# Fixed slots and an urgent first gather for the sample's index tiles, a third key/value buffer, counts by immediates, and a norm step with scalars

## The chip, the cores and the metric

The kernel runs on one core of one Trainium2 chip. The core has a matrix engine (TensorE, "PE" in the profile; "PEld" is its loading of stationary tiles), a vector engine (VectorE, "DVE"), a scalar engine (ScalarE, "ACT"), a general engine (GpSimd, "POOL") and a queue that issues most transfers (SyncE, "SP"). Each engine works through its own list of instructions in order and waits on semaphores for the others. The metric is the device time of one execution in microseconds, lower is better. Times of a kernel are medians over several executions; the profile shows one further execution.

## What is computed

One decoder layer for 1024 prompt tokens and for 8 sequences of 4 sample tokens that have 8192 cached tokens each. The inputs are normalised and projected once for two parallel groups of heads. Group A attends to the 256 best keys that a small "indexer" picks, group B is a retention with a running state. Both are gated, joined, projected, normalised, added to the input, and a gated embedding is added.

```python
def _rmsnorm(x, g):
    xf = x.astype(jnp.float32)
    y = xf * lax.rsqrt(jnp.mean(xf * xf, axis=-1, keepdims=True) + EPS) * g.astype(jnp.float32)
    return y.astype(x.dtype)

def _index_select(qi, wi, ki, qpos, kpos, topk):
    s = jnp.einsum('bqhd,bsd->bqhs', qi.astype(jnp.float32), ki.astype(jnp.float32)) * (D_IDX ** -0.5)
    score = jnp.einsum('bqh,bqhs->bqs', wi.astype(jnp.float32), jax.nn.relu(s))
    valid = kpos[None, None, :] <= qpos[None, :, None]
    score = jnp.where(valid, score, -jnp.inf)
    top_val, top_idx = lax.top_k(score, topk)
    return top_idx, jnp.isfinite(top_val)

def _dsa_sample(qa, ka, va, qi, ki, wi, cache_k, cache_v, cache_kidx, page_table, rel_bias):
    ...
    ki_past = cache_kidx[page_table].reshape(B, past, D_IDX).astype(ki.dtype)
    ki_all = jnp.concatenate([ki_past, ki], axis=1)
    ...
    idx, ok = _index_select(qi, wi, ki_all, qpos, kpos, topk)
    ...
```

## The kernel before

Matrix products are done in float32 by three products of split operands (`xh`, `xl` and `whi`, `wlo`): a weight block is loaded as `wraw`, cast by ACT to `whi` (L179), and POOL subtracts to get `wlo` (L181, four instructions for each half of a block). The program lists what is to be done; a scheduler that knows the dependences and the buffers sets the order on each engine, mostly by the order of the code. A tile belongs to a pool and a tag; a tag has a number of buffers, and an instruction that writes a reused buffer waits for the buffer's last readers, a store among them.

The stages that matter here, in order of time:

- *Start.* Nine blocks of tokens are loaded and normalised. `rstd_of` (L233) computes the inverse root of the mean square: ACT's `Sqrt`, a reciprocal, and one Newton step on DVE (L241 to L244, tiles of 128x1). The row is scaled (L532), transposed by PE into `pt` (L223) and split into `xh` (ACT, L228) and `xl` (DVE, L229). The same helper serves the output norm in `finish_y` (L1691).
- *Projections.* `proj_b` (L248) runs three matmuls per 128 rows of weights over three groups of tokens (`GRP`: 384, 384 and 288). Its results `pb` are consumed by `use_qa`, `use_ka`, `use_va`, `use_ga`. `use_kv` (L402) copies the keys or values of a group to `kvs` (ACT, L406), transposes them on PE (`kvt`, L410), copies them back (DVE, L412) and stores them. `kvs`, `kst`, `qst` and `sga` share the tag `qst` with two buffers.
- *Prompt selection.* Scores of the prompt's blocks are summed on DVE (L502) and masked by POOL (`score`, L504). `bisect_prompt` (L631) finds the 256th largest score of each row bit by bit. It copies the upper halves of the scores to 16 bits (`mask`, L668, one copy a block), counts once against zero, and then makes 15 rounds. A round counts six blocks: the two longest on ACT (`js`, L657), the others on DVE (`jk`, L661). ACT's sums of signs become counts by one step on the two columns (L665, with a constant table `cst`). Then `gb` (L680) and the next candidate `cand` (L682) follow. Every count of the next round waits for `cand`.
- *Sample index.* 16 gathers (L799, one per half of a sequence) bring cached index keys to `kx`, two buffers. PE transposes each in two halves (`ptx`, L809), ACT copies a half to `kT` (L810), PE multiplies it by the index queries (`pox`, L813), ACT applies the ReLU to `rl` (L816), and four `rl` are summed over heads with the weights `wst` on PE (`py`, L772 and L775), copied to `ys` (L777), stored, and transposed to `xe` (L784, L788). All these tiles come from the pool `sx` with rotating tags. The loop also advances the bisection and the rest of the projections (`unit`). Ahead of the loop stand `wst` (L756, from `wcol`) and the newest keys' scores: `pn`, `rn` (L762), `newsc` (L763 to L766).

Of the kernel before, what the change touches and what calls it, by code (L numbers as in the profile page):

```python
# [10 lines left out]
F32 = mybir.dt.float32  # L11
F32R = mybir.dt.float32r
# [108 lines left out]
def tile_step(ctx: ExitStack, tc: tile.TileContext, I, O):  # L121
# [32 lines left out]
    def C(name, rows=128):  # L154
        o, w = _CW[name]
        return cst[:rows, o:o + w]
# [76 lines left out]
    def rstd_of(ss, rows, scale, name, sp):  # L233

        v = sp.tile(list(ss.shape), F32, tag="rs_v", bufs=2, name=f"rv_{name}")
        nc.vector.tensor_scalar(v[:rows], ss[:rows], scale, EPS, op0=ALU.mult, op1=ALU.add)
        y = sp.tile(list(ss.shape), F32, tag="rs_y", bufs=2, name=f"ry_{name}")
        z = sp.tile(list(ss.shape), F32, tag="rs_z", bufs=2, name=f"rz_{name}")
        nc.scalar.activation(y[:rows], v[:rows], AF.Sqrt)
        nc.vector.reciprocal(y[:rows], y[:rows])  # L240
        nc.vector.tensor_tensor(z[:rows], y[:rows], y[:rows], op=ALU.mult)  # L241
        nc.vector.tensor_tensor(z[:rows], z[:rows], v[:rows], op=ALU.mult)
        nc.vector.tensor_scalar(z[:rows], z[:rows], -0.5, 1.5, op0=ALU.mult, op1=ALU.add)
        nc.vector.tensor_tensor(y[:rows], y[:rows], z[:rows], op=ALU.mult)  # L244
        return y
# [155 lines left out]

    def use_kv(g, pt, outs, outp, new):  # L402

        t0, n = GRP[g]
        st = qsp.tile([128, 2, 384], F32, tag="qst", bufs=2, name="kvs")
        nc.scalar.copy(st[:, 0, :n], pt[:, :n])  # L406
        tp = bank("kvt", "t")
        for i in range(0, n, 128):
            rows = min(128, n - i)
            nc.tensor.transpose(tp[:rows, i:i + 128], st[:, 0, i:i + rows], ident)  # L410
        nb = min(n, T - t0)
        nc.vector.tensor_copy(st[:, 1, :nb], tp[:, :nb])  # L412
        tk = st[:, 1, :nb].rearrange("p (b c) -> p b c", c=128)
        nc.sync.dma_start(outp[0, 0, t0:t0 + nb].rearrange("(b p) n d -> p b (n d)", p=128), tk)
        if g == 2:
            nc.vector.tensor_copy(new, tp[:NS, 256:384])
            nc.sync.dma_start(outs.rearrange("o b t n d -> (o b t) (n d)"), new)
        return tk
# [49 lines left out]
    with pool("ix", side="right") as ix:  # L468
# [69 lines left out]

        warm = ix.tile([128, 1], F32, name="warm")
# [15 lines left out]
        def project(g):  # L555

            proj_b(wki, 0, 72, use_ki, (g,))
            qis = ix.tile([128, 8, 384], F32R, tag="qis", bufs=2, name=f"qis{g}")
# [72 lines left out]
    def bisect_prompt():  # L631
# [18 lines left out]
        def count(src, thr, op, scale=None):  # L650
# [12 lines left out]
            if scale:  # L663
                a = slice(NB - NA, NB)
                V.scalar_tensor_tensor(cnt[:, a], cnt[:, a], -0.5, C("halfn")[:, a], op0=ALU.mult, op1=ALU.add)  # L665
# [82 lines left out]
    sx = sxs.enter_context(pool("sx", side="right"))  # L748

    wcol = sx.tile([128, 8], F32, name="wcol")  # L750
    wst = sx.tile([128, 8, 32], F32, name="wst")
    nc.sync.dma_start(wi_d, wi[:NS, 8, :])
# [8 lines left out]
    rn = sx.tile([NS, 8, NS], F32, name="rn")  # L761
# [7 lines left out]
    def head_sum(b, rls):  # L769
# [6 lines left out]
        ys = sx.tile([128, 512], F32, tag="ys", bufs=2, name="ys")  # L776
# [4 lines left out]
    def by_key(b, ys):  # L781
# [3 lines left out]
        xe = sx.tile([128, 4, 4, 4, 4], F32, tag="xe", bufs=1, name="xe")  # L785
# [9 lines left out]
    for b in range(8):  # L795
        rls = []
        for a in range(2):
            kx = sx.tile([128, 2048], F32, tag="kx", bufs=2, name="kx")
            nc.gpsimd.indirect_dma_start(  # L799
                out=kx, out_offset=None, in_=pages,  # L800
                in_offset=bass.IndirectOffsetOnAxis(ap=kidx[:, a * 8 + b:a * 8 + b + 1], axis=0))
            for up in range(2):
                pt = pair("ptx")
                kT = sx.tile([128, 1024], F32, tag="kT", bufs=2, name="kT")
# [10 lines left out]
                rl = sx.tile([128, 512], F32, tag="rl", bufs=6, name="rl")  # L815
# [1012 lines left out]
```

## Time and profile before

| | us |
|---|---|
| median of 3 runs | 1053.49 |
| lowest and highest | 1051.36, 1053.96 |
| the profiled execution's own time | 1057.99 |
| its span, first to last instruction | 1056.2 |
| granted PE clock, mean over the span | 0.977 |

The profiled execution lies 4.5 us above the median, and 1.8 us of its time lie outside the span. A group of the profile is written as line, engine, operation, the tile written and the tiles read (buffer numbers left out). In a timeline a row has the start, the duration, what ran, how often, and in brackets how long the engine had idled and what ended that. In a table of stretches PEclk is the clock that PE was granted, 1.00 being full.

### The profile page before, as it was taken

Reading aid. Unit: us, or ns where it says so; the run is one execution under the profiler, and the core shown is the slowest. Engines: PE = TensorE matmul, PEld = TensorE weight load, DVE = VectorE, ACT = ScalarE, POOL = GpSimd, SP = SyncE. Lnnn points to the kernel's source line nnn. Section 1 sums busy time; section 2 is a strip of 40 time slices with the busy share of each in tenths; the row PEclk is TensorE's granted clock in tenths of the full one; section 3 lists DMA queues with packets and bytes.
Section 4 is the critical chain, followed back from the end, with each engine's and each line's share of the span. In section 5 each row is a group of like instructions: output and inputs, shape, how many; then the busy total and the mean of one; then the engine's idle time right before and its main releaser. Section 6 shows DMA issues by size and latency. Waiting matters only on the chain.

```text
span 1056.2 us, 19867 instructions
## 1 busy us (share of the span) xinstructions
PE 994.1 (94%) x7375; PEld 836.9 (79%) x7375; DVE 678.7 (64%) x2022; ACT 504.2 (48%) x1092; POOL 322.6 (31%) x425
## 2 busy tenths in 40 slices
PE   4999998998999799998999996899999999999998
PEld 3999997766776798887888883566665899999998
DVE  6847678888492466977959937687754423773332
ACT  6546455876434377632252435556644523442211
POOL 4204123120301433525644512544330432232200
PEclk9999998998999899999999996999999999999999
DMA  8211236545353311202201724523211312432211
GB/s 294 66 60 51 95 96 208 185 130 173 123 165 108 74 42 41 61 23 87 65 22 52 180 75 136 151 76 107 79 56 42 117 41 81 136 126 87 82 38 40
DMA packets 98309, 102.24 MB, mean 97 GB/s; under 512 B 21346, under 2 KB 88386, under 8 KB 95906
## 3 DMA queue, kind: packets, MB, share of 16 engines
q1 hardware_dynamic: 92450, 74.74, 23.6%
q0 software_dynamic: 5760, 26.22, 7.9%
q8 instruction: 58, 0.95, 0.4%
q14 instruction: 41, 0.34, 0.1%
HBM read 79.25 MB, written 21.68 MB: 96 GB/s over the span
## 4 chain that ended last, share of the span: by engine, by line
PE 44%; DVE 5%; DMA 2%; POOL 2%; issue 2%; ACT 1%; SPq 0%; ACTq 0%; POOLq 0%; DVEq 0%
PE ptp L1596 4%; PE ob L1604 4%; PE pg L267 3%; PE pg L269 3%; PE pg L268 3%; PE po L267 3%; PE po L268 3%; PE po L269 3%; PE sa L1580 2%; PE sa L1581 2%; PE pvg L268 1%; PE pvg L269 1%; PE pvg L267 1%; PE pty L1651 1%; POOL wlo_vgb L181 1%
## 5 line engine op out<-in xcount | busy, mean ns | idle before, releaser
L1159 POOL DMA_INDIRECT kvs<-in_cache_kv,idx x64 | 66.7, 1042 | 78.8 <-ACT pT L1601 31.7
L267 PE MATMUL pqk<-whi_qkb,xh 128*128 128x256 f32 x256 | 75.1, 293 | 4.4 <-DVE rp L1038 4.3
L267 PE MATMUL pvg<-whi_vgb,xh 128*128 128x256 f32 x256 | 75.5, 295 | 0.5 <-ACT whi_qkb L179 0.4
L268 PE MATMUL pqk<-wlo_qkb,xh 128*128 128x256 f32 x256 | 74.3, 290 | 0.0
L268 PE MATMUL pvg<-wlo_vgb,xh 128*128 128x256 f32 x256 | 74.2, 290 | 0.0
L269 PE MATMUL pqk<-whi_qkb,xl 128*128 128x256 f32 x256 | 73.9, 289 | 0.0
L267 PE MATMUL po<-whi_o,yTh 128*128 128x256 f32 x256 | 73.2, 286 | 0.4 <-ACT yTh L1646 0.4
L269 PE MATMUL pvg<-whi_vgb,xl 128*128 128x256 f32 x256 | 73.5, 287 | 0.0
L267 PE MATMUL pg<-whi_g,yTh 128*128 128x256 f32 x256 | 72.7, 284 | 0.0
L269 PE MATMUL po<-whi_o,yTl 128*128 128x256 f32 x256 | 72.7, 285 | 0.0
L268 PE MATMUL po<-wlo_o,yTh 128*128 128x256 f32 x256 | 72.7, 284 | 0.0
L269 PE MATMUL pg<-whi_g,yTl 128*128 128x256 f32 x256 | 72.3, 283 | 0.0
L268 PE MATMUL pg<-wlo_g,yTh 128*128 128x256 f32 x256 | 72.2, 282 | 0.0
L1589 ACT ACTIVATE L<-L,mn 128x128 f32<-128x128 f32 (+7 forms) x64 | 49.6, 778 | 17.6 <-DVE mn L1586 17.0
L267 PEld LDWEIGHTS pqk<-whi_qkb,xh 128*128 128x128 f32 x256 | 49.4, 193 | 8.2 <-issue 3.5
L502 DVE SCALAR_TENSOR_TENSOR score<-r,wi,score 128x384 f32<-128x384 f32 (+5 forms) x42 | 41.0, 976 | 23.0 <-ACT r L498 21.7
L1785 DVE TENSOR_TENSOR sgm<-pu,sgm 128x256 f32<-128x256 f32 x32 | 13.6, 424 | 64.3 <-PE pu L269 60.6
L181 POOL TENSOR_TENSOR wlo_g<-wraw_g,whi_g 128x256 fp32r<-128x256 f32 x32 | 27.2, 881 | 87.4 <-ACT whi_g L179 87.3
L799 POOL DMA_INDIRECT kx<-in_cache_kidx,kidx x16 | 15.9, 995 | 116.7 <-PE ptx L809 115.8
L269 PEld LDWEIGHTS pqk<-whi_qkb,xl 128*128 128x128 f32 x256 | 49.5, 193 | 2.6 <-issue 2.4
L498 ACT ACTIVATE r<-si 128x384 f32<-128x384 f32 (+5 forms) x48 | 36.3, 758 | 32.0 <-PE si L356 30.6
L267 PEld LDWEIGHTS pvg<-whi_vgb,xh 128*128 128x128 f32 x256 | 48.5, 189 | 3.5 <-issue 0.8
(545 smaller groups left out, 3332.6 us busy)
## 6 DMA issues: line engine op xcount, KB each, us to landing
wraw_qkb<-in_w_in SPq DMA_DIRECT2D x16, 256.0 KB
wraw_vgb<-in_w_in SPq DMA_DIRECT2D x16, 256.0 KB
wraw_o<-in_w_out SPq DMA_DIRECT2D x8, 512.0 KB
qas<-qas_d SPq DMA_DIRECT2D x8, 512.0 KB
xr<-in_x_prompt SPq DMA_DIRECT2D x8, 512.0 KB
wraw_g<-in_w_ple_gate SPq DMA_DIRECT2D x8, 512.0 KB
out_y_prompt<-sgm SPq DMA_DIRECT2D x32, 128.0 KB
qas_d<-qst SPq DMA_DIRECT2D x8, 384.0 KB
```

What stands on the lines that cost most here:

```text
L181: nc.gpsimd.tensor_tensor(lo[:, a * 4 + k, :n], raw[:, k, :n], hi[:, a * 4 + k, :n].bitcast(F32), op=ALU.subtract)
L267: nc.tensor.matmul(pt[:, :n], ah, hi[:, k, :n], start=(k == 0), stop=False)
L268: nc.tensor.matmul(pt[:, :n], ah, lo[:, k, :n], start=False, stop=False)
L269: nc.tensor.matmul(pt[:, :n], al, hi[:, k, :n], start=False, stop=(k == kc - 1))
L498: nc.scalar.activation(r[:, :n], s[:, :n], AF.Relu)
L502: nc.vector.scalar_tensor_tensor(sc, r[:, :n], wi[:, qb, h:h + 1], sc, op0=ALU.mult, op1=ALU.add)
L1159: return nc.gpsimd.indirect_dma_start(out=dst, out_offset=None, in_=kvflat, in_offset=bass.IndirectOffsetOnAxis(ap=idx, axis=0))
L1580: nc.tensor.matmul(s[:, :wc], qas[:, h, :], kah[kv][:, c:c + wc], start=True, stop=False)
L1581: nc.tensor.matmul(s[:, :wc], qas[:, h, :], kal[kv][:, c:c + wc], start=False, stop=True)
L1589: behind[0] = nc.scalar.activation(L[:, :n], L[:, :n], AF.Exp, bias=least, scale=-1.0, accum_out=sm[:, i4:i4 + 1])
L1596: nc.tensor.transpose(tp[:, i4 * 128:i4 * 128 + 128], P[i4][:, kb * 128:kb * 128 + 128], ident)
L1604: nc.tensor.matmul(ob[64 * o:64 * o + 64, :256], vtok[:, kb, kv * 64:kv * 64 + 64], pT[:, o * 256:o * 256 + 256], start=(kb == 0), stop=(k ...
```

## The change

Four edits:

- *Norm step.* Of the three steps with two operands two are fused into one with two scalar operands read per partition, and the third takes its second factor as such a scalar.
- *Third key/value buffer.* For the middle group of tokens `kvs` gets a tag of its own, `kvx`, in the pool `sx`.
- *Counts by immediates.* The step that turns ACT's two sums into counts becomes two steps of one column, each with its constants in the instruction.
- *Sample's index tiles.* `rn`, `xe` and every rotating tile get a fixed slot, all made at the head of the stage in a set order (the first use of a tag takes the tile made then). The order in which they are made sets where they lie. The first two gathers have no wait of their own left, where before they waited for the last readers of the memory under them. The first gather is issued under high priority.

Beside these, the buffer `qis0` is made some lines earlier.

```diff
-        nc.vector.tensor_tensor(z[:rows], y[:rows], y[:rows], op=ALU.mult)
-        nc.vector.tensor_tensor(z[:rows], z[:rows], v[:rows], op=ALU.mult)
+        nc.vector.tensor_scalar(z[:rows], y[:rows], y[:rows], v[:rows], op0=ALU.mult, op1=ALU.mult)
         nc.vector.tensor_scalar(z[:rows], z[:rows], -0.5, 1.5, op0=ALU.mult, op1=ALU.add)
-        nc.vector.tensor_tensor(y[:rows], y[:rows], z[:rows], op=ALU.mult)
+        nc.vector.tensor_scalar(y[:rows], y[:rows], z[:rows], None, op0=ALU.mult)
...
+    sxp = []
+
     def use_kv(g, pt, outs, outp, new):
 
         t0, n = GRP[g]
-        st = qsp.tile([128, 2, 384], F32, tag="qst", bufs=2, name="kvs")
+        st = (sxp[0].tile([128, 2, 384], F32, tag="kvx", bufs=1, name="kvs") if g == 1 else
+              qsp.tile([128, 2, 384], F32, tag="qst", bufs=2, name="kvs"))
...
+        qfirst = ix.tile([128, 8, 384], F32R, tag="qis", bufs=2, name="qis0")
...
             if scale:
-                a = slice(NB - NA, NB)
-                V.scalar_tensor_tensor(cnt[:, a], cnt[:, a], -0.5, C("halfn")[:, a], op0=ALU.mult, op1=ALU.add)
+                for j in range(NB - NA, NB):
+                    V.tensor_scalar(cnt[:, j:j + 1], cnt[:, j:j + 1], -0.5, (j + 3) * 64.0, op0=ALU.mult, op1=ALU.add)
...
     sx = sxs.enter_context(pool("sx", side="right"))
+    sxp.append(sx)
+
+    made = {}
+
+    def slot(tag, shape, name):
+        if tag in made:
+            return made.pop(tag)
+        return sx.tile(shape, F32, tag=tag, bufs=1, name=name)
 
     wcol = sx.tile([128, 8], F32, name="wcol")
     wst = sx.tile([128, 8, 32], F32, name="wst")
+    rn = sx.tile([NS, 8, NS], F32, name="rn")
+    made["xe"] = sx.tile([128, 4, 4, 4, 4], F32, tag="xe", bufs=1, name="xe")
+    for tag, w in (("ys0", 512), ("ys1", 512), *((f"rl{i}", 512) for i in range(1, 6)), ("kT1", 1024),
+                   ("kx1", 2048), ("rl0", 512), ("kT0", 1024), ("kx0", 2048)):
+        made[tag] = sx.tile([128, w], F32, tag=tag, bufs=1, name=tag)
+    turn = {"rl": 0, "kT": 0, "kx": 0, "ys": 0}
+
+    def ring(tag, w, n):
+        i = turn[tag] % n
+        turn[tag] += 1
+        return slot(f"{tag}{i}", [128, w], tag)
+
...
-            kx = sx.tile([128, 2048], F32, tag="kx", bufs=2, name="kx")
-            nc.gpsimd.indirect_dma_start(
-                out=kx, out_offset=None, in_=pages,
-                in_offset=bass.IndirectOffsetOnAxis(ap=kidx[:, a * 8 + b:a * 8 + b + 1], axis=0))
+            kx = ring("kx", 2048, 2)
+            with (tc.high_priority() if b + a == 0 else nullcontext()):
+                nc.gpsimd.indirect_dma_start(
+                    out=kx, out_offset=None, in_=pages,
+                    in_offset=bass.IndirectOffsetOnAxis(ap=kidx[:, a * 8 + b:a * 8 + b + 1], axis=0))
             for up in range(2):
                 pt = pair("ptx")
-                kT = sx.tile([128, 1024], F32, tag="kT", bufs=2, name="kT")
+                kT = ring("kT", 1024, 2)
...
-                rl = sx.tile([128, 512], F32, tag="rl", bufs=6, name="rl")
+                rl = ring("rl", 512, 6)
```

`ys` and `xe` are taken in the same way. The edits also move instructions. On POOL, at the entry of the sample's index, the order before was this (`score` is the select of a prompt block, `kx` a gather, `wlo_ga` one half of the split of the first gate weights):

```order
L504 AFFINE_SELECT score<-score 128x128 x2
L799 DMA kx<-in_cache_kidx,kidx 128x2048 x2
L181 TENSOR_TENSOR wlo_ga_1923<-wraw_ga_1924,whi_ga_1922 128x256 x4
L181 TENSOR_TENSOR wlo_ga_1923<-wraw_ga_1931,whi_ga_1922 128x256 x4
L799 DMA kx<-in_cache_kidx,kidx 128x2048 x6
```

The same place on POOL in the changed kernel:

```order
L506 AFFINE_SELECT score<-score 128x128
L181 TENSOR_TENSOR wlo_ga_1922<-wraw_ga_1923,whi_ga_1921 128x256 x4
L822 DMA kx_1725<-in_cache_kidx,kidx 128x2048
L506 AFFINE_SELECT score<-score 128x128
L822 DMA kx_1722<-in_cache_kidx,kidx 128x2048
L181 TENSOR_TENSOR wlo_ga_1922<-wraw_ga_1930,whi_ga_1921 128x256 x4
L822 DMA kx<-in_cache_kidx,kidx 128x2048 x6
```

The first half of the split moved ahead of the first gather, and the last block's select moved between the two gathers. On DVE, at the same place, before (`mask` is the copy of the last block's scores, `jk` the passes of the first count):

```order
L668 COPY mask<-score 128x1024
L763 TENSOR_TENSOR rn<-rn,wi 32x256
L337 SCALAR_TENSOR_TENSOR qst<-pb,qst 64x384
L661 TENSOR_SCALAR jk,cnt<-mask 128x1024
L764 TENSOR_REDUCE newsc<-rn 32x32
L661 TENSOR_SCALAR jk,cnt<-mask 128x896
L765 TENSOR_TENSOR newsc<-newsc,cst 32x32
L661 TENSOR_SCALAR jk,cnt<-mask 128x768
L766 TENSOR_TENSOR newsc<-newsc,cst 32x32
L661 TENSOR_SCALAR jk,cnt<-mask 128x640
L337 SCALAR_TENSOR_TENSOR qst<-pb,qst 64x256
```

And on DVE in the changed kernel:

```order
L785 TENSOR_TENSOR rn<-rn,wi 32x256
L786 TENSOR_REDUCE newsc<-rn 32x32
L336 SCALAR_TENSOR_TENSOR qst<-pb,qst 64x256
L392 TENSOR_SCALAR qs<-pb 64x32 x2
L787 TENSOR_TENSOR newsc<-newsc,cst 32x32
L788 TENSOR_TENSOR newsc<-newsc,cst 32x32
L427 TENSOR_TENSOR kst<-pb,kst 128x384
L779 TENSOR_TENSOR wst<-wcol,cst 128x256
L671 COPY mask<-score 128x1024
L664 TENSOR_SCALAR jk,cnt<-mask 128x1024
L664 TENSOR_SCALAR jk,cnt<-mask 128x896
```

The last block's copy and the whole first count moved behind the newest keys' scores, `kst` and `wst`. On ACT, from the two casts of the gate weights on, before:

```order
L179 CAST whi_ga_1922<-wraw_ga_1924 128x1024
L179 CAST whi_ga_1922<-wraw_ga_1931 128x1024
L336 ACTIVATE qst<-pb 64x256 x2
L657 ACTIVATE js,cnt<-mask,cand 128x1024
L810 COPY kT<-ptx 128x1024
L657 ACTIVATE js,cnt<-mask,cand 128x896
L810 COPY kT<-ptx 128x1024
L424 CAST kst<-pb 128x384
L816 ACTIVATE rl<-pox 128x512
```

And on ACT in the changed kernel:

```order
L179 CAST whi_ga_1921<-wraw_ga_1923 128x1024
L179 CAST whi_ga_1921<-wraw_ga_1930 128x1024
L335 ACTIVATE qst<-pb 64x256
L784 ACTIVATE rn<-pn 32x256
L335 ACTIVATE qst<-pb 64x256
L426 CAST kst<-pb 128x384
L408 COPY kvs<-pb 128x384
L660 ACTIVATE js,cnt<-mask,cand 128x1024
L660 ACTIVATE js,cnt<-mask,cand 128x896
L833 COPY kT_1724<-ptx 128x1024
```

`rn`, `kst` and `kvs` moved ahead of the first `js`, and both `js` of the first round stand ahead of the first `kT`.

More of the change, by code (lines that the diff above doesn't have):

```diff
@@ L1 @@
 import math
-from contextlib import ExitStack
+from contextlib import ExitStack, nullcontext
 import numpy as np
@@ L557, in project @@
             proj_b(wki, 0, 72, use_ki, (g,))
-            qis = ix.tile([128, 8, 384], F32R, tag="qis", bufs=2, name=f"qis{g}")
+            qis = qfirst if g == 0 else ix.tile([128, 8, 384], F32R, tag="qis", bufs=2, name=f"qis{g}")
             qiss.append(qis)
@@ L760, in tile_step @@
         nc.tensor.matmul(pn[:NS, h * 32:h * 32 + 32], qsn[:, h, :], kis, start=True, stop=True)
-    rn = sx.tile([NS, 8, NS], F32, name="rn")
     nc.scalar.activation(rn, pn[:NS, :256].rearrange("p (h k) -> p h k", h=8), AF.Relu)
@@ L775, in head_sum @@
                 nc.tensor.matmul(py[32 * i:32 * i + 32, :], wst[:, b, :], rls[i], start=True, stop=True)
-        ys = sx.tile([128, 512], F32, tag="ys", bufs=2, name="ys")
+        ys = ring("ys", 512, 2)
         nc.scalar.copy(ys, py)
@@ L784, in by_key @@
             nc.tensor.transpose(pt[:, i * 128:(i + 1) * 128], ys[:, i * 128:(i + 1) * 128], ident)
-        xe = sx.tile([128, 4, 4, 4, 4], F32, tag="xe", bufs=1, name="xe")
+        xe = slot("xe", [128, 4, 4, 4, 4], "xe")
         pv = pt.rearrange("p (r i e) -> p r i e", r=4, i=4)
```

## The prediction

> **What bounds the kernel now.** I read the page's busy shares first, then a table of stretches, then the timeline of each engine inside the stretches in which TensorE (PE) has gaps.
>
> ```profile
> span 1056.2 us, 19867 instructions
> PE 994.1 (94%) x7375; PEld 836.9 (79%) x7375; DVE 678.7 (64%) x2022; ACT 504.2 (48%) x1092; POOL 322.6 (31%) x425
> ```
>
> PE works for 994.1 of 1056.2 us. The change adds and removes no matmul, so it can only act on the 62 us in which PE idles and on the clock that PE is granted after idling. Next, a table of stretches that the edited code touches (from and to; length; busy time and instructions of PE, its weight loads, DVE, ACT and POOL; PE's clock; DMA share; GB/s).
>
> ```profile
> 0.00:22.00 22.00, 7.78 (x29) 5.91 (x30) 13.88 (x35) 13.84 (x27) 10.37 (x18) 1.00 0.89 286
> 178.00:186.00 8.00, 6.04 (x18) 2.49 (x19) 7.71 (x22) 7.43 (x13) 0.28 (x1) 0.57 0.89 320
> 238.00:243.00 5.00, 2.50 (x9) 0.62 (x7) 4.76 (x16) 4.54 (x8) 0.96 (x1) 0.75 0.82 242
> 243.00:248.00 5.00, 4.84 (x20) 2.73 (x24) 3.70 (x15) 4.81 (x9) 0.00 (x0) 0.57 0.90 263
> 902.00:924.00 22.00, 21.09 (x181) 20.70 (x180) 18.40 (x58) 10.60 (x31) 7.89 (x9) 1.00 0.45 142
> ```
>
> Read PE's busy time against the length, then the clock. The start leaves PE empty for 14 us. Around 180 and 240 PE waits, and its clock falls to 0.57 to 0.75 for some microseconds. Around 910 there is under 1 us to win. The three waits in the middle, as PE's timeline has them:
>
> ```profile
> 175.11 1.94 PE L809 MATMUL ptx<-cst,kx 128*128 128x128 f32 x16 [1.09 <-DMA kx<-in_cache_kidx,kidx]
> 179.96 1.97 PE L813 MATMUL pox<-kT,qbd 128*64 128x512 f32 x4 [2.91 <-ACT kT L810]
> 213.06 0.81 PE L410 MATMUL kvt<-cst,kvs 128*128 128x128 f32 x3 [2.76 <-ACT kvs L406]
> 240.96 1.98 PE L813 MATMUL pox<-kT,qbd 128*64 128x512 f32 x4 [2.43 <-DVE vnew L416]
> ```
>
> The first index tile comes late and its copy `kT` later; at 213.06 a key/value copy is late; at 240.96 a VectorE (DVE) copy. Each part of the change aims at one of these or at the start.
>
> **The urgent gather and the late count.** Before, GpSimd (POOL) and the cast on ScalarE (ACT) that it waits for do this:
>
> ```profile
> 167.27 0.29 POOL L504 TENSOR_SCALAR_AFFINE_SELECT score<-score 128x128 f32<-128x128 f32 x1 [20.94 <-DVE score L502]
> 168.14 1.38 POOL L799 DMA_INDIRECT kx<-in_cache_kidx,kidx  x1 [0.57 <-issue]
> 169.67 2.00 ACT L179 CAST whi_ga<-wraw_ga 128x1024 fp32r<-128x1024 f32 x2 [1.36 <-PE pb L258]
> 170.80 5.58 POOL L181 TENSOR_TENSOR wlo_ga<-wraw_ga,whi_ga 128x256 fp32r<-128x256 f32 x8
> ```
>
> The changed order puts half of that weight split, four of the eight, **ahead** of the first gather, and the last score block's select behind the gather. The split waits for the cast, which waits for PE, so it cannot start before 170.80 whatever its place. Its half takes 5.58 / 2 = 2.79, so the first gather is issued at about 173.6 instead of 168.14, 5.5 us later, in spite of its urgency. From issue to PE's use it took 175.11 - 168.14 = 6.97, so `ptx` starts near 180.6. The select follows gather (1.38) and gaps near 175.5.
>
> On DVE the mask copy of that block and the whole first count now stand behind nine other steps, from `rn` (the newest keys' score) to `wst`.
>
> ```profile
> 167.82 0.69 DVE L668 COPY mask<-score 128x1024 bf16<-128x1024 bf16 x1
> 168.43 0.40 DVE L763 TENSOR_TENSOR rn<-rn,wi 32x256 f32<-32x256 f32 x1
> 177.44 0.16 DVE L676 TENSOR_SCALAR cand<-tbits 128x6 int32<-128x6 int32 x1
> 181.21 0.42 DVE L756 TENSOR_TENSOR wst<-wcol,cst 128x256 f32<-128x256 f32 x1
> 169.00:177.00 8.00, 5.32 (x12) 1.00 0.85 290
> ```
>
> The nine (first and last are the second and fourth row) sum to about 3.6 us; in the new order `rn` can begin near 172.5, when ACT has passed the two casts and two short copies, so the mask copy starts near 176.1. Mask 0.69, the count 5.32 (the last row: the count's line alone, six passes and six readouts), 0.5 of small steps: first `cand` at 182.6 against 177.44, **5.2 us later**. ACT's order then has two `js` passes, not one, ahead of the first `kT`:
>
> ```profile
> 177.63 1.15 ACT L657 ACTIVATE js<-mask,cand 128x1024 bf16<-128x1024 bf16 x1 [2.36 <-DVE cand L676]
> 178.90 1.01 ACT L810 COPY kT<-ptx 128x1024 f32<-128x1024 f32 x1
> 179.80 1.04 ACT L657 ACTIVATE js<-mask,cand 128x896 bf16<-128x896 bf16 x1
> ```
>
> 178.90 - 177.63 = 1.27 and then 1.04 put `kT` at 184.9; `pox` follows 1.06 behind it as before, at 186.0 against 179.96: PE loses **6.0 us** here, and the landing at 180.6 is not what decides. What hid the gather before is gone; `kT` is late because of the count.
>
> **The third key/value buffer.** Only the middle token group of the key and value projections gets it.
>
> ```profile
> 212.61 0.40 ACT L406 COPY kvs<-pb 128x288 f32<-128x288 f32 x1 [1.59 <-DMA out_k_prompt<-kvs]
> 201.39 0.53 SPq L426 DMA_DIRECT2D ka_d<-kst  x1
> 205.44 0.39 SPq L414 DMA_DIRECT2D out_k_prompt<-kvs  x1
> 190.76 0.49 PE L410 MATMUL kvt<-cst,kvs 128*128 128x128 f32 x3
> 213.80 3.31 PE L813 MATMUL pox<-kT,qbd 128*64 128x512 f32 x8
> 186.78 1.08 PE L813 MATMUL pox<-kT,qbd 128*64 128x512 f32 x4
> ```
>
> The copy at 212.61 waited for the store issued at 205.44, which took 7.17. Now that copy waits for the `ka_d` store of 201.39, four microseconds older. If it too took 7.17 it is done at 208.6, and PE reaches the transpose at 213.06 - 2.76 = 210.3. So the 2.76 goes, and with it the slow stretch behind it: 0.81 - 0.49 on the transposes and 3.31 - 2 x 1.08 on `pox`, some 1.5. Together 4.3 on PE's own path.
>
> **The count by immediates.** Fifteen two-operand steps become thirty one-operand ones.
>
> ```profile
> 232.32 5.56 POOL L181 TENSOR_TENSOR wlo_ga<-wraw_ga,whi_ga 128x256 fp32r<-128x256 f32 x8
> 234.16 3.75 DVE L665 SCALAR_TENSOR_TENSOR cnt<-cnt,cst 128x2 f32<-128x2 f32 x1 [0.82 <-ACT js L657]
> 240.54 0.27 DVE L416 COPY vnew<-kvt 32x128 f32<-32x128 f32 x1
> L665 DVE SCALAR_TENSOR_TENSOR cnt<-cnt,cst x15: 153/160/3745, 181.5 to 252.1; 128x2 f32<-128x2 f32 x15
> ```
>
> One of fifteen lasted 3745 ns instead of 160, to the end of POOL's run of eight subtractions (232.32 + 5.56 = 237.88), and `vnew`, which PE waits for at 240.96, is queued behind it. The new step has one input from memory. But `cand` two steps on still has two, and falls into the same POOL run. Bounds for what it will wait: 0, or all that is left of the run, about 3.2. The norm's rows below show two-input steps beside POOL at 0.65 and 0.73; they are the many, 3745 the one, so I take 0.6: **3.0 saved** on DVE. Against it 12 rounds up to `vnew` with a second small step, 0.1 each: +1.2. The Trainium skill (SBUF — State Buffer, "Who interferes with whom") says that a DVE instruction with two SBUF inputs contends with a GpSimd instruction that reads SBUF and that the loser waits for the whole instruction. By that rule a wait is at most one subtraction, 5.56 / 8 = 0.70, the 3745 ns are not explained, and the sum would be the one taken here.
>
> **DVE's loop sets the exit.** DVE, ACT and PE are tied round by round here, so the later of two paths counts. DVE's own waits between 178 and 244 (total, times, longest):
>
> ```profile
> DVE cnt L665 <- ACT js L657: 3.5, 5, 1.4
> DVE kvs L412 <- PE kvt L410: 0.8, 1, 0.8
> ```
>
> DVE up to `vnew`: +5.2 entry; -0.8, since `wst` (0.42) and `kst`, put at the same, now lie ahead of the count; -3.0 +1.2 from above; and of the 4.3 us in these two rows I take 2.6 as gone, the 0.8 with PE's gap and half of the 3.5, since the second `js` no longer stands behind `kT` in the first round: **0.0**. Bounds: none of them gone (+2.6), all gone (-1.7). PE's own path: +6.0 -4.3 -2.43 = -0.7, so DVE decides and the stage ends where it did.
>
> **The norm step.** Three two-operand steps become two with a scalar operand.
>
> ```profile
> 12.55 0.73 DVE L241 TENSOR_TENSOR rz_x<-ry_x 128x1 f32<-128x1 f32 x1
> 13.31 0.65 DVE L242 TENSOR_TENSOR rz_x<-rz_x,rv_x 128x1 f32<-128x1 f32 x1
> 13.99 0.15 DVE L243 TENSOR_SCALAR rz_x<-rz_x 128x1 f32<-128x1 f32 x1
> 14.18 0.46 DVE L244 TENSOR_TENSOR ry_x<-ry_x,rz_x 128x1 f32<-128x1 f32 x1
> 17.15 1.94 PE L223 MATMUL pt<-cst,score 128*128 128x128 f32 x8 [3.89 <-DVE xl L229]
> ```
>
> The stretched rows stand beside POOL's work; the 0.15 row, with one memory input, does not stretch. The new third chain is three steps at some 0.19 pitch, 0.57 against 14.18 + 0.46 - 12.55 = 2.09 before: up to 1.5 earlier, and PE waits at 17.15 for what follows it. At least 0, if a scalar read from memory stretches as well. I take **-1.2**, since the first projection also needs ACT and weights. The second use, around 910, lies in a stretch with 0.9 idle: -0.3.
>
> **Sum** against the profiled execution's own 1057.99: 0.0 - 1.2 - 0.3 = -1.5, 1056.5. That execution lay 4.5 above the median of the three runs, 1053.49; taken from the median the forecast is **1052.0**.
>
> **Rivals.**
> - *Starved to the end of a POOL run (slower).* The 3745 row ended where the run ended. If that is the rule for small two-input steps, `rn` and its followers slip behind 173.6, `wst` then meets POOL's second half (from about 177.0) and waits to 179.8: first `cand` at 186.3, 3.7 later than above, and `cand` of round 12 loses 2.6 again. -1.5 + 3.7 + 2.6 = +4.8: 1058.3. It decides once `wst` is reached after the second half has begun. For it: the one row. Against it: the norm's rows. If only the later `cand` is held: -1.5 + 2.6, 1054.6.
> - *The loop gives back more (faster).* All 4.3 of waits go (-1.7 more), and with no gap at 240 the clock stays up through 243 to 248, where 4.84 us ran at 0.57 (up to 2.1): 1052.0 - 3.8 = 1048.2. For it: DVE and ACT start the loop with work already done. Against: ACT is busy 7.43 of 8.
> - *The buffer wait changes place.* The `ka_d` store is later than I think and the gap of 2.76 stays: PE's path becomes +2.1 and decides: 1054.1. Here the change doesn't do what it says. Against: the store is four microseconds older.
>
> **How the numbers follow.** Forecast 0.38 (own range 1049.8 to 1053.8), starved 0.17, only `cand` held 0.17, faster loop 0.20, buffer wait 0.08. A measurement of this kernel tells some 0.3% (3.2 us) from no change: faster means under 1050.3, slower over 1056.7. Faster: the faster loop and a third of the forecast's case, 0.32. Slower: the starved case and a little of the next, 0.20. Same: 0.48. The range reaches to the outer rivals, 1047.5 to 1058.3.
>
> **What would show it.** In the new profile the first `kx` gather starts behind four `wlo_ga` steps near 172.5 to 174, and the first `cand` some 5 us later than before, counted from the end of the preceding projection; `pox` waits about 9 us in all. The wait of `kvt` for `kvs` is gone. No `cnt` step lasts over 0.3; the `cand` beside the second `wlo_ga` run says which rival holds. The norm rows at 12 us are 0.15 each. I am wrong if POOL reaches the gather before the split, if the stage ends more than 3 us from where it did, or if stretches that no edit touches move.

## The result, and the profile after

| | before | after |
|---|---|---|
| median, us | 1053.72 (6 runs, 1050.99 to 1056.21) | 1063.3 (6 runs, 1058.84 to 1064.79) |
| ratio after to before, 95% interval | | 1.0088 [1.0068, 1.0108] |
| profiled execution: time, span, clock | 1057.99, 1056.2, 0.977 | 1064.56, 1062.5, 0.972 |

The change makes the kernel 9.6 us slower; the forecast was 1.5 faster, and its slowest rival 1058.3. The page of the changed kernel, its first two lines:

```profile
span 1062.5 us, 19864 instructions
PE 994.0 (94%) x7375; PEld 840.5 (79%) x7375; DVE 673.2 (63%) x2019; ACT 505.1 (48%) x1092; POOL 322.1 (30%) x425
```

PE is busy as long as before, 994.0 against 994.1, so what the span is longer by is idle time of PE. The same stretches as before, in the changed kernel:

```profile
0.00:22.00 22.00, 8.76 (x33) 6.88 (x34) 12.41 (x32) 13.86 (x27) 10.87 (x18) 1.00 0.88 284
178.00:186.00 8.00, 2.52 (x12) 2.55 (x13) 7.79 (x23) 2.67 (x5) 2.36 (x4) 0.50 1.02 394
238.00:243.00 5.00, 5.00 (x33) 4.97 (x32) 4.18 (x11) 4.16 (x6) 3.86 (x6) 1.00 0.46 115
243.00:248.00 5.00, 4.58 (x31) 2.51 (x30) 4.46 (x16) 4.86 (x8) 3.62 (x5) 1.00 1.02 354
902.00:924.00 22.00, 22.00 (x194) 21.11 (x194) 13.70 (x44) 10.85 (x30) 8.95 (x9) 1.00 0.39 127
```

The first row shows PE busy 1.0 longer at the start and the last one 0.9 longer in the finish: there the norm edit does what it should. The second row shows where the loss begins: between 178 and 186 PE is busy 2.52 of 8 us instead of 6.04. PE's timeline in the changed kernel, its waits of over 0.5 us between 183 and 251:

```profile
183.48 3.64 PE L832 MATMUL ptx<-cst,kx 128*128 128x128 f32 x16 [9.09 <-DMA kx<-in_cache_kidx,kidx]
190.18 1.08 PE L836 MATMUL pox<-kT,qbd 128*64 128x512 f32 x4 [0.95 <-ACT kT L833]
199.67 1.07 PE L832 MATMUL ptx<-cst,kx 128*128 128x128 f32 x8 [2.11 <-DMA kx<-in_cache_kidx,kidx]
226.31 0.52 PE L412 MATMUL kvt<-cst,kvs 128*128 128x128 f32 x3 [1.75 <-DVE xe L810]
250.42 1.08 PE L836 MATMUL pox<-kT,qbd 128*64 128x512 f32 x4 [0.71 <-DVE xe L810]
```

PE waits 9.09 for the first gather. What led there, on POOL, DVE and ACT of the changed kernel:

```profile
171.27 3.02 POOL L181 TENSOR_TENSOR wlo_ga<-wraw_ga,whi_ga 128x256 fp32r<-128x256 f32 x4 [21.22 <-ACT whi_ga L179]
174.47 1.14 POOL L822 DMA_INDIRECT kx<-in_cache_kidx,kidx  x1 [0.18 <-issue]
175.63 0.30 POOL L506 TENSOR_SCALAR_AFFINE_SELECT score<-score 128x128 f32<-128x128 f32 x1
183.57 0.16 DVE L679 TENSOR_SCALAR cand<-tbits 128x6 int32<-128x6 int32 x1
183.77 1.15 ACT L660 ACTIVATE js<-mask,cand 128x1024 bf16<-128x1024 bf16 x1 [3.82 <-DVE cand L679]
186.09 0.99 ACT L833 COPY kT<-ptx 128x1024 f32<-128x1024 f32 x1
```

Gather at 174.47 (forecast 173.6), `cand` at 183.57 (182.6), `kT` at 186.09 (184.9), first `pox` 7.2 later than before (6.0): the entry came nearly as forecast. Only the gather took longer, 9.0 from its issue to `ptx` where the forecast took 6.97. The loop then gave back far less than forecast, and a second loss stands at 650 us, where the first gap among the last stage's scores `sa` grew from 5.48 to 8.12. Before and after:

```profile
649.11 0.47 PE L1580 MATMUL sa<-kahi,qas 128*128 128x128 f32 x1 [5.48 <-DVE mn L1586]
```
```profile
655.82 0.48 PE L1603 MATMUL sa<-kahi,qas 128*128 128x128 f32 x1 [8.12 <-DVE mn L1609]
```

### The profile page after: what moved, and what is told of

Same layout as the page of the kernel before. It is cut to its first block, busy times and chain, and to the rows that moved or that the text cites. A ratio compares the mean times of both kernels' runs of the same rounds, so it can differ in the third digit from the quotient of the medians.

```text
span 1062.5 us, 19864 instructions
## 1 busy us (share of the span) xinstructions
PE 994.0 (94%) x7375; PEld 840.5 (79%) x7375; DVE 673.2 (63%) x2019; ACT 505.1 (48%) x1092; POOL 322.1 (30%) x425
## 4 chain that ended last, share of the span: by engine, by line
PE 44%; DVE 6%; DMA 2%; ACT 2%; POOL 1%; issue 1%; SPq 0%; ACTq 0%; DVEq 0%; POOLq 0%
PE ob L1627 4%; PE ptp L1619 4%; PE po L266 3%; PE pg L266 3%; PE po L267 3%; PE po L268 3%; PE pg L268 3%; PE pg L267 3%; PE sa L1603 2%; PE sa L1604 2%; PE pty L1674 1%; PE oS L1409 1%; PE pvg L267 1%; PE pvg L268 1%; PE pvg L266 1%
```

## The experiments

**One edit at a time.** Each of the first three is the kernel before with one edit; the fourth is the changed kernel without one.

norm_alone, the norm step alone (`rstd_of`, three steps with two operands become two with scalars):

> The kernel before with the norm step's edit alone. Theory A (the edit frees DVE time at the start, the scheduler then puts half of the gate weights' split ahead of the first gather and the whole first count behind the newest keys' scores, and that late entry is what the change costs): slower than before by 5 to 9 us, ratio 1.005 to 1.009; the first cand comes some 6 us late and PE waits 9 to 11 us in all ahead of the first pox, while the waits for kvs and vnew of the kernel before stay or shrink. Theory B (the loss comes from the fixed slots and the urgent gather): 0 to 2 us faster, ratio 0.998 to 1.000, first pox not later than before.

all_but_norm, the other edits without it:

> The changed kernel with the old norm step. Its order has the gathers ahead of the split and one kT ahead of the first js. Theory A: faster than before by 4 to 9 us, ratio 0.991 to 0.996; the first pox follows the key projection by about 3 us instead of 6, and the waits of PE for kvs and vnew are gone. Theory B: still slower than before by 5 us or more, ratio over 1.005.

cnt_alone, the counts by immediates alone:

> The kernel before with the counts by immediates alone; its order is the old one but for these steps. If a two-input step held to the end of a POOL run is what delays vnew, the gap of 2.4 us ahead of pox near 241 goes, cand beside that run waits at most 0.7: 1 to 4 us faster, ratio 0.996 to 0.999. If cand is now held as cnt was, no change: 0.999 to 1.001.

kvx_alone, the third key/value buffer alone:

> The kernel before with the third key/value buffer alone. The wait of kvt for kvs (2.8 us near 213) goes. If PE's own path counts, 3 to 4 us faster, ratio 0.996 to 0.997; if DVE's loop sets the exit, under 1 us, 0.999 to 1.000. Its order also has the output of the sample's states (sso) moved ahead of the last head norm on DVE, as in the changed kernel: if that costs what it seemed to there, the wait of sa near 650 is 8 us instead of 5.5, which takes back up to 2.6 us.

| run | median us | ratio, 95% interval |
|---|---|---|
| norm_alone | 1059.87 | 1.0074 [1.0048, 1.0099] |
| all_but_norm | 1054.69 | 1.0019 [0.9999, 1.0038] |
| cnt_alone | 1052.17 | 0.9985 [0.9962, 1.0008] |
| kvx_alone | 1054.08 | 1.0007 [0.9985, 1.0029] |

Nearly the whole loss comes with the norm edit, whose rows lie ahead of 42 us and behind 900. The other edits together gain nothing that can be measured, though a gain was expected of them: all_but_norm lies between the ranges of both theories.

**Is it POOL's order?** In norm_alone POOL has the half split ahead of the first gather, as in the changed kernel. norm_old_entry keeps the norm edit and puts POOL back; entry_flipped has no edit and turns POOL's order over. `got` are the gathers, `s` a subtraction of `load_w`. Here and below `NoSync` and `Sync` are short for a dependence that sets an order on one engine, and for one with a semaphore between engines.

```diff
+                if name == "ga0" and a == 0:                # norm_old_entry
+                    tc.add_manual_dep(s.ins, got[1].name, NoSync)
...
+                if name == "ga0" and a * 4 + k == 3:        # entry_flipped
+                    tc.add_manual_dep(got[0], s.ins.name, NoSync)
```

> The kernel before with the norm edit, and one added order: the four subtractions of the first half of wlo_ga (the first gate weights) stand behind the second gather on POOL, as they did before. POOL's order is then that of the kernel before throughout; on ACT and DVE some steps of the entry stay where the norm edit moved them. Theory A (the norm edit costs through the entry order that it brings about, not by its own steps): first pox of PE within 2 us of 180, no gap of over 4 us ahead of the first ptx or pox; ratio 0.998 to 1.003 (the VectorE sum sso is still early here, which theory C below prices at 2.4 us). Theory B (the norm edit costs elsewhere, by its own steps or by later orders): still 1.005 to 1.009.

> The kernel before with none of the four edits and one added order: the first gather stands behind the first half of the wlo_ga subtractions on POOL, as in the changed kernel. Theory A (entry order): the first two gathers are issued near 173 instead of 168, PE loses 4 to 8 us up to its first pox, and 3 to 5 us are left of it at 338 us; with sso early as well, ratio 1.004 to 1.009. Theory B (the entry order alone is covered by the loop's slack): at most 2 us are left at 338, ratio 0.999 to 1.003.

norm_old_entry: 1061.53 us, 1.0068 [1.0045, 1.0090]; entry_flipped: 1065.81, 1.0093 [1.0061, 1.0126]. The first refutes theory A in this form: POOL's order is back and the time is not. Its first `pox` is only some 2 us late (table below), so most of its loss arises behind the entry. And the gather is still late, as its POOL shows:

```profile
171.57 0.29 POOL L508 TENSOR_SCALAR_AFFINE_SELECT score<-score 128x128 f32<-128x128 f32 x1 [21.44 <-DVE score L506]
172.44 1.16 POOL L803 DMA_INDIRECT kx<-in_cache_kidx,kidx  x1 [0.57 <-ACT whi_ga L181]
```

The gather follows the last score block's select again, but the select itself waits for DVE's last score step until 171.57; before, it ran at 167.27. The second run shows that POOL's order costs as well if it alone is turned over:

```profile
168.08 0.29 POOL L509 TENSOR_SCALAR_AFFINE_SELECT score<-score 128x128 f32<-128x128 f32 x1 [20.94 <-DVE score L507]
171.60 2.83 POOL L183 TENSOR_TENSOR wlo_ga<-wraw_ga,whi_ga 128x256 fp32r<-128x256 f32 x4 [3.23 <-ACT whi_ga L181]
174.61 1.14 POOL L804 DMA_INDIRECT kx<-in_cache_kidx,kidx  x1 [0.17 <-issue]
```

POOL idles 3.23 with the gather behind it. In both the gather is late, by two ways.

**Where do the late scores come from?** From PE's own order. The first of the four matmuls of the last prompt scores (`si`), in the kernel before and then in the changed one:

```profile
163.67 0.39 PE L355 MATMUL si<-kih,qis 128*128 128x512 f32 x1
```
```profile
167.51 0.39 PE L354 MATMUL si<-kih,qis 128*128 128x512 f32 x1
```

Before, the last `si` stands behind 14 of 24 matmuls of the projection of the second token group; after, behind all 24 and 12 of the next group. That is 10 x 0.177 + 12 x 0.134 = 3.4 us of `pb` matmuls (their pitch in the same timelines). In the second half of the stage each `si` group stands about where the next but one stood before. Whether this makes the loss is told by a table of places, `NEXT`, that puts every `si` group between the same two `pb` matmuls as in one of the two kernels; nothing else is touched:

```diff
+        for m, (p, i) in zip(si, NEXT):
+            edge(m[0], (pbs[p][i - 1] if i else pbs[p - 1][-1]))
+            edge(pbs[p][i], m[-1])
```

norm_scores_placed is norm_alone with the places of the kernel before; before_scores_late is the kernel before, without any of the edits, with the places that the norm edit brings.

> The kernel before with the norm edit, and one table of orders on PE: every group of prompt-score matmuls (si) stands between the same two projection matmuls (pb) as in the kernel before. POOL's order at the entry, DVE's from there on and the place of sso are then as before without any further edge. Theory E (the norm edit costs because the last si stands 22 projection matmuls later on PE, which makes the last score, the gathers and the first count late): the last score step of DVE ends within 1.5 us of 167.2 (169.6 with the norm edit alone), first pox within 2 us of 180, gap ahead of the first sa 5 to 6; ratio 0.997 to 1.002. Theory B (the norm edit's own steps or something else it moves): 1.005 to 1.009, as with the norm edit alone and with only POOL's order put back.

> The kernel before with none of the four edits, and one table of orders on PE: every group of prompt-score matmuls stands between the projection matmuls at which it stands with the norm edit, the last one 22 of them later than before. POOL then has the half split ahead of the first gather, and sso comes early on DVE, by themselves. Theory E: the last score step ends at 169 to 172, the first pox comes 4 to 9 us later than 180, ratio 1.004 to 1.010. Theory B (the norm's own steps are needed for the loss): 0.998 to 1.003.

| run | last score step | first gather | first `cand` | first `pox` | ratio, 95% interval |
|---|---|---|---|---|---|
| before (both profiles) | 165.9, 166.2 | 168.1, 168.4 | 177.4, 177.7 | 180.0, 180.2 | 1 |
| norm_alone | 168.3 | 173.0 | 181.1 | 184.8 | 1.0074 [1.0048, 1.0099] |
| norm_old_entry | 170.2 | 172.4 | 182.1 | 182.1 | 1.0068 [1.0045, 1.0090] |
| entry_flipped | 166.7 | 174.6 | 179.7 | 192.0 | 1.0093 [1.0061, 1.0126] |
| after (both profiles) | 170.0, 170.9 | 174.5, 175.3 | 183.6, 187.1 | 187.1, 190.6 | 1.0088 [1.0068, 1.0108] |
| before_scores_late | 169.9 | 174.6 | 182.7 | 186.7 | 1.0098 [1.0070, 1.0127] |
| norm_scores_placed | 164.0 | 166.2 | 175.5 | 178.0 | 0.9937 [0.9917, 0.9958] |

Each row is one execution: that of entry_flipped took 5.7 us more than the run's median, that of norm_scores_placed 4.8 less.

Theory E is shown from both sides. With the scores late and no edit at all a loss as large is there; with the norm edit and the scores in place the kernel is faster than before by 6.6 us (1047.24), which is more than theory E itself had. POOL's order at the entry and the place of `sso` followed the scores in both runs without an edge of their own. In norm_scores_placed:

```profile
161.76 0.39 PE L374 MATMUL si<-kih,qis 128*128 128x512 f32 x1
164.01 1.28 DVE L522 SCALAR_TENSOR_TENSOR score<-r,wi,score 128x1024 f32<-128x1024 f32 x1 [0.82 <-ACT r L518]
166.23 1.38 POOL L819 DMA_INDIRECT kx<-in_cache_kidx,kidx  x1 [0.57 <-issue]
```

The score is read as a chain: `si` on PE, `r` on ACT, `score` on DVE, the select and then the gather on POOL.

The late scores do not cost by the entry alone. In before_scores_late and in norm_alone a later step of DVE, `gb`, is held for 6.09 (more on this below), and PE waits 3.73 and 3.74 behind it. In before_scores_late:

```profile
238.98 5.55 POOL L181 TENSOR_TENSOR wlo_ga<-wraw_ga,whi_ga 128x256 fp32r<-128x256 f32 x8
238.47 6.09 DVE L701 TENSOR_SCALAR gb<-cnt 128x6 int32<-128x6 f32 x1
248.92 1.97 PE L834 MATMUL pox<-kT,qbd 128*64 128x512 f32 x4 [3.73 <-DVE gb L701]
```

The changed kernel's two profiles and that of norm_old_entry have no such wait. So the size of the loss is put together differently in each of these kernels.

**The place of `sso`.** The sum `sso` of the last head pair (L1145, two steps and a scaling) stood behind that pair's norm chain on DVE and now stands inside it, where it waits for PE. no_norm_sso_back is all_but_norm with `sso` put back; sso_early_alone is the kernel before with `sso` put early.

```diff
+            for s in (sso if hp == 3 else ()):              # no_norm_sso_back
+                tc.add_manual_dep(s, zi.ins.name, NoSync)
...
+            for s in (sso if hp == 3 else ()):              # sso_early_alone
+                tc.add_manual_dep(yi.ins, s.name, NoSync)
```

> The changed kernel without the norm edit, and the sum sso of the last head pair put back behind that pair's norm chain on DVE, as in the kernel before; little else moves. Theory C (sso early makes the chain late and PE waits for it at sa): the gap ahead of the first sa is 5 to 6 us instead of 8.1, and the time falls by 2 to 4 us against all_but_norm: ratio 0.995 to 0.999. Theory D (the wait only changes place, a later one takes it): gap shorter, time as all_but_norm, 1.000 to 1.004.

> The kernel before with one added order: the last head pair's gy product stands behind the sum sso on DVE, so that sso waits for PE ahead of the norm chain; nothing else of weight moves. Theory C: gap ahead of the first sa 7.5 to 8.5 instead of 5.48, ratio 1.001 to 1.004. Theory D: ratio 0.999 to 1.001.

The first `sa` gap, in sso_early_alone and then in no_norm_sso_back:

```profile
649.35 0.48 PE L1587 MATMUL sa<-kahi,qas 128*128 128x128 f32 x1 [7.85 <-DVE mn L1593]
```
```profile
647.43 0.47 PE L1611 MATMUL sa<-kahi,qas 128*128 128x128 f32 x1 [5.71 <-DVE mn L1617]
```

The gap goes with the order. In time, early `sso` gave 1.0019 [0.9994, 1.0044], and putting it back went from all_but_norm's 1.0019 to 0.9990 [0.9971, 1.0008]. Both point to 2 or 3 us, as theory C had it; neither interval excludes theory D by itself.

**Was the long count step chance?** The forecast counted a `cnt` step of 3745 ns as 3.0 to be won. A second profile of the kernel before:

> The kernel before, once more, for a second profile of the same orders. Theory H (DVE's cnt step of 3745 ns beside the wlo_ga run, which the forecast counted as 3.0 to be won, is a chance of the execution shown): here it takes under 1 us, vnew starts near 236 to 237 instead of 240.5, and the first pqk at 332 to 335 instead of 338.1. Theory I (it belongs to the order): 3 to 6 us again, and vnew after 239.5.

```profile
234.96 0.33 DVE L665 SCALAR_TENSOR_TENSOR cnt<-cnt,cst 128x2 f32<-128x2 f32 x1 [0.74 <-ACT js L657]
235.33 0.68 DVE L680 TENSOR_SCALAR gb<-cnt 128x6 int32<-128x6 f32 x1
236.04 0.66 DVE L682 SCALAR_TENSOR_TENSOR cand<-gb,cand 128x6 int32<-128x6 int32 x1
```

The same step beside the same POOL run (233.75 to 239.34) took 0.33. Theory H holds for the step: the order alone does not bring the 3745 ns. `vnew` (238.9) and the first `pqk` (335.7) came later than theory H had them. This execution took 1053.86 us, the median; the one shown before took 4.1 more. In sso_early_alone, whose order here is that of the kernel before, the step took 0.33 too. But it was held a second time, in entry_flipped, whose POOL run stands at 248.97 to 254.53:

```profile
250.80 3.74 DVE L670 SCALAR_TENSOR_TENSOR cnt<-cnt,cst 128x2 f32<-128x2 f32 x1 [0.82 <-ACT js L662]
```

In before and in entry_flipped the step began 1.84 and 1.83 after the start of POOL's run; in before_again, sso_early_alone and norm_scores_placed 1.20 to 1.21 after it, and took 0.33 or 0.34. So in these five profiles the hold goes with the moment at which the step meets the run. No experiment moved that moment alone, and why it differs between two executions of one order is open.

**A hold in six of the kernels.** In no_norm_sso_back another step of DVE meets the run's start, and is held to the end of the run, 228.19 + 5.56. POOL, DVE and PE:

```profile
228.19 5.56 POOL L181 TENSOR_TENSOR wlo_ga<-wraw_ga,whi_ga 128x256 fp32r<-128x256 f32 x8
227.88 5.90 DVE L686 SCALAR_TENSOR_TENSOR cand<-gb,cand 128x6 int32<-128x6 int32 x1
237.99 1.51 PE L837 MATMUL pox<-kT,qbd 128*64 128x512 f32 x4 [3.58 <-DVE gb L684]
```

all_but_norm has the same 5.90, all_four_orders_back (below) 5.91. In kvx_alone it is `gb`, as in norm_alone and before_scores_late:

```profile
227.61 5.56 POOL L181 TENSOR_TENSOR wlo_ga<-wraw_ga,whi_ga 128x256 fp32r<-128x256 f32 x8
227.10 6.10 DVE L683 TENSOR_SCALAR gb<-cnt 128x6 int32<-128x6 f32 x1
```

gated_split lets the run wait until this `cand` is done; no instruction changes its place.

```diff
+    tc.add_manual_dep(subs["ga1", 0], cands[20].name, Sync)
```

> The changed kernel without the norm edit and with sso put back (the run no_norm_sso_back, 0.999), and one added wait: POOL starts the wlo_ga subtractions of the loop's second run only when DVE has finished the candidate step cand of round 11, which there began 0.3 us before the run and took 5.90 us, to its end. No instruction changes its place. Theory F (the hold is on the path that PE waits for ahead of pox at 238, gap 3.6): that cand takes at most 1 us, the steps of the next round 0.6 to 0.9 each, the gap falls to at most 1.5, and the time falls by 2 to 4 us to a ratio of 0.995 to 0.998. Theory G (what DVE gains is lost again before PE needs it, or the next round is held as long): gap 3 or more or a new one of that size within 30 us, ratio 0.998 to 1.001.

In gated_split:

```profile
228.66 5.57 POOL L183 TENSOR_TENSOR wlo_ga<-wraw_ga,whi_ga 128x256 fp32r<-128x256 f32 x8
228.35 0.15 DVE L688 SCALAR_TENSOR_TENSOR cand<-gb,cand 128x6 int32<-128x6 int32 x1
233.61 0.65 DVE L688 SCALAR_TENSOR_TENSOR cand<-gb,cand 128x6 int32<-128x6 int32 x1
238.36 1.08 PE L840 MATMUL pox<-kT,qbd 128*64 128x512 f32 x4 [0.43 <-DVE cnt L671]
```

`cand` takes 0.15, the next one 0.65, PE's gap falls from 3.58 to 0.43, and the time from 1053.52 to 1049.24 us: 0.9948 [0.9927, 0.9968]. Theory F holds, with a little more than it had. POOL's run begins 0.95 behind the start of its gather with the wait and without it, so the trace shows no delay of POOL. The hold had thus taken away what the other edits gain. The wait alone, on the kernel before, was not run.

**All edits, repaired.** all_four_orders_back is the changed kernel with the scores in place and `sso` put back; all_repaired has the gate as well. after_again is a second profile of the changed kernel.

> The changed kernel, all four edits in place, with two orders put back: the si groups on PE as above, and sso behind the last head pair's norm chain. Theory E: the loss of the changed kernel is these two orders alone, and what stays is the norm's microsecond at the start and the earlier entry of the slots: ratio 0.993 to 1.000, first pox before 178. Theory B: still over 1.004.

> The changed kernel, all four edits in place, with the scores placed on PE as before, sso put back, and the second run of wlo_ga subtractions waiting for the cand of round 11. By the runs so far: all_four_orders_back 0.9993, less what the gate gave (0.9990 to 0.9948, 0.0042): 0.995, some 1048.5 us; 0.992 to 0.997 if the two add. If what is gained is lost again behind, 0.997 to 1.000.

> The changed kernel once more, for a second profile of the same orders. If its entry is the order's doing, the last score step starts at 169 to 171, the first gather at 173.5 to 175.5, the first pox at 186 to 188.5 again, and the gap ahead of the first sa is 8 again; the slow clock at 816 to 836 (0.59 to 0.84 where the kernel before shows 1.00) may go.

all_four_orders_back: 1052.77 us, 0.9993 [0.9971, 1.0016]. all_repaired: 1048.08, 0.9960 [0.9941, 0.9978]. With the two orders back the whole loss of the changed kernel, 9.6 us, is gone, and the hold (5.91 in all_four_orders_back, gone in all_repaired) costs about 3.5 more; the intervals of these two runs just overlap. The kernel before and the changed one are both beaten by three versions, whose intervals overlap: norm_scores_placed, gated_split and all_repaired. after_again took 1063.70 us, with the scores, the gather and the `sa` gap (8.11) as expected; the slow clock near 816 to 836 came again (0.71 from 828 to 832), and before_again has it too (0.60 from 816 to 820). Its first `pox`, at 190.6, came later than that, and its first `cand` 3.5 later than in the first profile, through a hold at the entry. On DVE:

```profile
177.06 0.42 DVE L779 TENSOR_TENSOR wst<-wcol,cst 128x256 f32<-128x256 f32 x1
177.39 3.85 DVE L671 COPY mask<-score 128x1024 bf16<-128x1024 bf16 x1
181.27 1.22 DVE L664 TENSOR_SCALAR_CACHE_REDUCE jk<-mask 128x1024 bf16<-128x1024 bf16 x1
```

## Why the forecast was wrong, and where it was right

How much later a matmul starts on PE in the changed kernel, in us, against the second profile of before (1053.86 us, at the median), for both profiles after:

| place (time in before_again) | after | after_again | forecast |
|---|---|---|---|
| last `pb` of the query weights, ahead of the entry (169.7) | +0.2 | +1.1 | -1.2 |
| first `pox` (180.2) | +6.9 | +10.4 | +4.8 |
| first `pqk`, behind the loop (335.7) | +6.2 | +7.9 | -1.2 |
| last 64x128 transpose into `ret`, ahead of the `sa` gap (630.0) | +5.2 | +6.6 | -1.2 |
| `ob`, behind the `sa` gap (654.2) | +7.7 | +9.0 | -1.2 |
| end (1052.1) | +10.4 | +9.7 | -1.5 |

- **The step that failed: "DVE decides and the stage ends where it did", 0.0.** Against its 5.2 at the entry the forecast set 3.0 from the counts and 2.6 from waits (and small steps of -0.8 and +1.2). Of that, DVE's time from the first `cand` to `vnew` gave back 61.27 - 61.68 = -0.4 (after) and 1.4 (after_again) against before_again. The 3.0 were a hold that the second profile of the same kernel lacks, and the gap of 2.43 at 240.96 that PE's own path was to gain stood behind the same hold; before_again has 1.34 there, ahead of a `pxt`. PE's waits from the first `pox` to the first `pqk`, from which the forecast took 2.76 and 2.43, sum to 8.2 in before_again, 8.1 in after and 5.8 in after_again: new ones came, 2.11 and 1.50 for a later gather and 1.75 for `xe`. The sum was set against the median, though its terms were read off an execution 4.5 us above it, and part of that surplus (2.4 us by the first `pqk`) lay in these very terms.
- **The step that was missing.** The forecast compared the orders of POOL, DVE and ACT at the entry and not PE's in the stage ahead of it. It put the late gather down to the split, and the whole to the slots; the cause is the place of the scores on PE, and the edit that moves them is the norm step, priced at -1.2 there. The likewise unread order at 650 us, `sso`, costs some 2.4 in both profiles (from 5.2 to 7.7, from 6.6 to 9.0).
- **The entry** was right in its order of steps and nearly in size: `pox` 7.2 later in the two first profiles, forecast 6.0. That the landing of the gather does not decide was wrong: with 9.0 for the gather, `ptx` is done at 187.13, and `kT`, behind the count, at 187.08. In after_again, whose count is held at its start, `kT` alone decides (a wait of 3.46).
- **The third buffer.** The wait of `kvt` for `kvs` is gone, as forecast, but 1.75 of it stands at 226.31, behind `xe`. That is the rival "changes place" in part, though not by the late store that it named.
- **The counts.** No `cnt` lasts over 0.155 us now, and beside the run `cand` took 0.66, about what the forecast took, and `gb` 0.85, which it had not counted. Alone the edit gave 0.9985 [0.9962, 1.0008].
- **The norm step** was right in mechanism, nearly right in size at the start and too small in the finish. In the changed kernel:

```profile
9.84 0.27 DVE L241 TENSOR_SCALAR rz_x<-ry_x,rv_x 128x1 f32<-128x1 f32 x1
10.15 0.15 DVE L242 TENSOR_SCALAR rz_x<-rz_x 128x1 f32<-128x1 f32 x1
10.34 0.21 DVE L243 TENSOR_SCALAR ry_x<-ry_x,rz_x 128x1 f32<-128x1 f32 x1
```

  The rows are 0.27 and 0.21, not 0.15, but do not stretch. From PE's first transpose to its first projection matmul both profiles of before take 10.84, after, after_again and norm_scores_placed 9.33, 9.47 and 9.41: 1.4 to 1.5 less (1.2 forecast). In the changed kernel this is lost again ahead of 169: PE waits 1.65 at 33.15 where before had 0.58, and its granted clock from 28 to 36 and from 36 to 44 us is 0.84 and 0.95 (after_again 0.94 and 0.85). before_again and norm_scores_placed have 1.00 there, the latter with the same wait of 1.66. In the finish, between the same two `po` matmuls, every profile with the edit is 1.1 to 1.2 shorter than the two of before (0.3 forecast), of which the two gaps of 0.27 and 0.64 are most.
- **The rival "starved to the end of a POOL run"** named the right danger at the wrong weight: it strikes in after_again (`mask`, 3.85) and in each profile of the kernels that led to the gate. The rule that the forecast weighed against it, from the Trainium skill (SBUF — State Buffer, "Who interferes with whom"), that the loser waits for the whole instruction, does not explain these holds: 5.90 and 6.10 are eight subtractions of 0.70, not one, though the 0.65 to 0.85 of other steps agree with it.

What stays open: why the scheduler moves the scores when the norm step changes; why a step at the same place of the same order is held in one execution and not in the next; and how the 6.6 us of norm_scores_placed divide beyond the 1.4 at the start and some 1.1 in the finish. The slots were not run alone.

## What to carry to other kernels

An edit of three tiny steps cost 7 to 8 us because a scheduler re-ordered another engine's work over 100 us later: after any edit compare the order on every engine, the busiest first, and pin what feeds the next stage's first transfer. A stall seen once in one profile is no term of a sum until a second profile of the same kernel shows it. And where short steps of one engine stretch beside a run of another, look for those that start just ahead of the run, and let the run wait for the step.

## What the runs showed of the hardware

- A DVE step can be held over a whole run of back-to-back POOL subtractions. It was 5.90 to 6.10 us, to within 0.05 of the run's end, in six profiles in which the step began 0.3 to 0.5 ahead of a run of eight. Two steps begun as far ahead were not held so long: a `gb` in norm_old_entry was free after 1.37 (0.50 ahead), and the `mask` copy in after took 1.21 (0.52 ahead of a run of four, which took 3.31 where that of after_again took 2.76). A `cnt`, `gb` or `cand` begun inside the run took at most 0.85 or, begun 1.84 and 1.83 after its start in before and in entry_flipped, 3.75 and 3.74, to the end.
- It is not only two-input steps: `gb` (128x6, one input) was held 6.10 in kvx_alone and `mask` (a copy, 128x1024) 3.85 in after_again, 0.57 past the end of a run of four. The counting passes (`jk`) beside the same runs kept their 0.6 to 1.0.
- It is the subtractions that hold, not the gather ahead of them: in gated_split `cand` began 0.64 behind the gather's start, as in no_norm_sso_back, and took 0.15.
